# Where the masks and exponentials of an mLSTM head's decays are computed: in the core of the head before, or in the head's own key and value projection

## The chip, the cores and the metric

The kernel runs on one core of a Trainium2 chip. A core has five engines that run their own queues of instructions and wait for each other through semaphores: TensorE (PE, matrix products, with PEld for its weight loads), VectorE (DVE), ScalarE (ACT), GpSimd (POOL) and SyncE (SP), which here issues DMAs. ACT issues some DMAs too. The metric is the time of one execution on the device in microseconds (us). The profile is one execution, recorded instruction by instruction.

## The reference

One layer of a backbone over 1024 latent tokens with a prefix of 256 context tokens, width 1024. After a modulated norm, an input projection feeds two branches, a bidirectional mLSTM with 4 heads (keys and queries of 128, values of 256) and a windowed attention with 16 heads. Their outputs are projected, gated, merged and added to the input, and a convolutional feed-forward part follows. The change lies in the mLSTM. In each direction, with chunks of 128 tokens, a head computes

```
C_t = f_t C_{t-1} + i_t k_t v_t^T        n_t = f_t n_{t-1} + i_t k_t
h_t = C_t^T q_t / max(|n_t . q_t|, exp(-m_t))
```

In chunked form a chunk's output is the sum of two products. One is with the state C that the earlier chunks left. The other is inside the chunk: the scores S = k q^T, each multiplied by a decay exp(u_t + g_s), where u and g come from sums of the gates, and only for s up to t (from t on in the backward direction). The limit is a mask that adds a large negative number ahead of the exponential. Both directions are added, normed per head, and multiplied by a sigmoid gate.

## The kernel before

All matrix products are taken in three parts: each fp32 operand is split into a high half (copied by ACT, line 44) and a low half (the rest, by DVE, line 49), and `mm3` issues high x high, high x low and low x high (lines 91 to 93). Weights come in four loads of two row blocks each; a load goes to one of two raw buffers (`w1r`) and is split into `w1h` and `w1l`, of which there are five of each. SP issues the loads; a load waits until its raw buffer's former content has been split.

`stage_mlstm` works head by head. For head h:

- `proj_kv(h)` makes k and v for 10 chunks: two context chunks are loaded, eight latent ones are products with 8 row blocks (24 matmuls of 128x384 each), in one of two PSUM buffers. ACT evacuates k and the high half of v (`VH`), DVE the low half (`VL`).
- `trans_k` transposes k; `states` makes the first two state updates of each direction: `kwh` on POOL (line 941), `kwl` on DVE (942), the matmuls dC, the new state C on DVE (947, 949), and its halves `CH` (ACT) and `CL` (DVE).
- `turn(h-1)` transposes the former head's output (`mt`), scales it on ACT (`mo`, line 1042) and stores it; `proj_q` projects the queries (w_mlqo); `branch_sums` loads, adds and stores operands of later stages, with loads on ACT's queue and stores on SP's.
- `core(h)` makes S, multiplies it by the decays `ub` (DVE, line 977) and splits the result. Then, step by step, it updates the states and makes the outputs: the matmuls o (inside the chunk) and i (with the state), `nm` on ACT (992) and small operations on DVE (993 to 997), `hf` on POOL (999) the first time a chunk is reached and on DVE (1001) the second. Each of the states and outputs hangs on the one before through a chain over PE, DVE and ACT.
- `proj_o(h)` projects the output gate (the matmuls `mo` into the tiles `sg`). Its matmuls are placed among the core's, where PE would otherwise wait.
- `decays(h+1)` prepares the next head's four tiles `ub` of 128x512: a DMA of rows of u on SP's queue (917), the addition of the mask on POOL (922, one per tile) and four exponentials of 128x128 on ACT per tile (924).
- `readout(h)`: the sigmoid of `sg` on ACT (1023), squares of `hf` with their sums (1027, `rj`), two small POOL operations that end in a power (1028, 1029, `rr`), and hf * rr * sg on DVE (1032). This is done for two halves of the tokens.

Order on each engine: a scheduler lists all instructions ahead of time and picks, engine by engine, by the order in the program and by estimated times. `tc.issue_after(x)` pins what is written inside it behind the instruction x. In `decays` the additions of the masks are pinned behind `E.kw`, which is the last `kwh` of the core. The program's order around the change, at the end of `stage_mlstm`, is: core, proj_o, decays of the next head, readout, proj_kv of the next head.

Of the kernel before, what the change touches and what calls it, by code (L numbers as in the profile page):

```python
# [2 lines left out]

# [7 lines left out]
AF = mybir.ActivationFunctionType  # L11
ALU = mybir.AluOpType
# [11 lines left out]
NCB = NCTX // P  # L24
NBLK = NT // P
# [4 lines left out]
DQK = 128  # L30
# [12 lines left out]
def copy_act(nc, out, in_, scale=1.0):  # L43
    return nc.scalar.activation(out, in_, AF.Copy, scale=scale)  # L44
# [41 lines left out]
def mm3(nc, ps, lhs, rhs, ls, rs, start=True, stop=True):  # L86
    n = len(lhs)
    for i in range(n):
        lh, ll = lhs[i]
        rh, rl = rhs[i]  # L90
        nc.tensor.matmul(ps, lh[:, ls], rh[:, rs], start=start and i == 0, stop=False)  # L91
        nc.tensor.matmul(ps, lh[:, ls], rl[:, rs], start=False, stop=False)  # L92
        nc.tensor.matmul(ps, ll[:, ls], rh[:, rs], start=False, stop=stop and i == n - 1)  # L93


def sl(a, n):
    return slice(a, a + n)
# [3 lines left out]
def layer_kernel(ctx: ExitStack, tc: tile.TileContext, A: dict, out: bass.AP, dbg=None):  # L101
# [76 lines left out]
    with ExitStack() as st:  # L178
        stage_mlstm(E, st)
# [514 lines left out]
def stage_mlstm(E, st):  # L694
    nc, tc, A, ident, expo, hT, wts, dr = E.nc, E.tc, E.A, E.ident, E.expo, E.hT, E.wts, E.dr
# [26 lines left out]
    def orders(h):  # L722
        f = list(range(NBLK))
        bk = [1, 0] + list(range(NBLK - 1, NCB - 1, -1))
        return [(0, f), (1, bk)] if h % 2 == 0 else [(1, bk), (0, f)]

    def v_tiles(h, j, src):
        vh = vp.tile([P, DVA], F32R, tag="VH", name=f"VH{h}_{j}")
        vl = vp.tile([P, DVA], F32R, tag="VL", name=f"VL{h}_{j}")
        nc.gpsimd.tensor_copy(vh[:, DV:DVA], ones2[:, 0:2])  # L730
        nc.gpsimd.tensor_copy(vl[:, DV:DVA], ones2[:, 2:4])
        split_from(nc, vh[:, 0:DV], vl[:, 0:DV], src)
        return vh, vl

    def proj_kv(h):
        w = wts.load(A["w_ml"][h], 384)
        ks, vs = [None] * NBLK, [None] * NBLK
        for j in orders(h)[0][1]:
            k = kp.tile([P, DQK], F32, tag="k", name=f"k{h}_{j}")
            if j < NCB:  # L740
                nc.sync.dma_start(k, E.kx_d[j][:, h * DQK : (h + 1) * DQK])
                vr = kp.tile([P, DV], F32, tag="vr", name=f"vr{h}_{j}", bufs=2)
                nc.sync.dma_start(vr, E.vx_d[j][:, h * DV : (h + 1) * DV])
                vs[j] = v_tiles(h, j, vr)
            else:
                ps = mm_tile(f"kv{h}_{j}")
                mm3(nc, ps[:, :384], hT, w, sl((j - NCB) * P, P), sl(0, 384))
                copy_act(nc, k, ps[:, 0:DQK], scale=DQK ** -0.5)
                vs[j] = v_tiles(h, j, ps[:, 128:384])
            ks[j] = k  # L750
            if h == 0 and j - NCB in (0, 3):
                branch_sums()
        H.setdefault(h, {}).update(k=ks, V=vs)

    def proj_q(h):
        w = wts.load(A["w_mlqo"][h], 384)
        H.setdefault(h, {})["wqo"] = w
        qT = []
        for t in range(2):
            ps = mm_tile(f"q{h}_{t}")  # L760
            mm3(nc, ps, w, hT, sl(0, DQK), sl(t * 512, 512))
            qh, ql = b512(f"qh{h}_{t}"), b512(f"ql{h}_{t}")
            split_from(nc, qh, ql, ps)
            qT.append((qh, ql))
        H[h]["qT"] = qT

    def trans_k(h):
        kT = []
        for t in range(2):
            pt = tp_tile(f"kT{h}_{t}")  # L770
            for c in range(4):
                nc.tensor.transpose(pt[:, c * P : (c + 1) * P], H[h]["k"][NCB + 4 * t + c], ident)
            kh, kl = b512(f"kh{h}_{t}"), b512(f"kl{h}_{t}")
            split_from(nc, kh, kl, pt)
            kT.append((kh, kl))
        H[h]["kT"] = kT

    def proj_o(h):
        w = H[h]["wqo"]
        sgs = [rp.tile([P, 4, DV], F32, tag="sg", name=f"sg{h}_{t}", bufs=2) for t in range(2)]  # L780
        for cc in range(NB) if h % 2 else range(NB - 1, -1, -1):
            ps = mm_tile(f"mo{h}_{cc}")
            mm3(nc, ps[:, :DV], hT, w, sl(cc * P, P), sl(DQK, DV))

            fn = AF.Sigmoid if h == MLH - 1 else AF.Copy
            nc.scalar.activation(sgs[cc // 4][:, cc % 4], ps[:, :DV], fn)
        H[h]["sg"] = sgs

    GC = {}
# [117 lines left out]

    DM = {}

    def decays(h):  # L910

        for i in range(2):
            for d, _ in orders(h):
                t = i ^ d
                u = DM[h, t, d] = wp.tile([P, 4, P], F32, tag="ub", name=f"ub{h}_{t}_{d}", bufs=4)
                r0 = d * 64 + h * NBLK + NCB + 4 * (t if d == 0 else 1 - t)
                nc.sync.dma_start(
                    u.rearrange("p c t -> p (c t)"),
                    GC["u_d"][r0 : r0 + 4].rearrange("r t -> (r t)")[None, :].to_broadcast([P, 4 * P]),
                )  # L920
                with tc.issue_after(E.kw.ins):
                    nc.gpsimd.tensor_tensor(u, u, mlmask[:, d, None, :].to_broadcast([P, 4, P]), op=ALU.add)
                for c in range(4):
                    nc.scalar.activation(u[:, c], u[:, c], AF.Exp, bias=GC["col"]("g", r0 + c))

    EARLY = 2

# [88 lines left out]
    def halves(h):  # L1016
        return (1, 0) if h % 2 == 0 else (0, 1)

    def readout(h):
        hf, sgs = H[h]["hf"], H[h]["sg"]  # L1020
        for t in halves(h):
            if h < MLH - 1:
                nc.scalar.activation(sgs[t], sgs[t], AF.Sigmoid)
            rr = rp.tile([P, 8], F32, tag="rr", name=f"rr{h}_{t}", bufs=2)
            for c in range(4):
                junk = rp.tile([P, 512], F32, tag="mo", name=f"rj{h}_{t}_{c}", bufs=2)
                nc.scalar.activation(junk[:, :DV], hf[:, 4 * t + c], AF.Square, accum_out=rr[:, c : c + 1])
            nc.gpsimd.tensor_scalar(rr[:, 0:4], rr[:, 0:4], 1.0 / DV, EPS, op0=ALU.mult, op1=ALU.add)
            nc.gpsimd.tensor_tensor(rr[:, 4:8], rr[:, 0:4], expo[:, 0:4], op=ALU.pow)
            for c in range(4):  # L1030
                x = hf[:, 4 * t + c]
                E.turned = nc.vector.scalar_tensor_tensor(x, x, rr[:, 4 + c : 5 + c], sgs[t][:, c], op0=ALU.mult, op1=ALU.mult)
# [17 lines left out]
    def branch_sums():  # L1050
        n, i = SUMS.pop(0)
        two = [rp.tile([P, 4, DV], F32, tag="sg", name=f"{n}{i}_{j}", bufs=2) for j in range(2)]
        x, y, z, w = [t.rearrange("p c d -> p (c d)")[:, o : o + 512] for t in two for o in (0, 512)]
        tt = nc.vector.tensor_tensor
        if n[0] == "s":
            wb = A["w" + n[1:]]
            for o, src in ((x, wb[0, :, i]), (y, wb[1, :, i]), (z, wb[1, :, i + 4]), (w, wb[0, :, i + 4])):
                nc.scalar.dma_start(o, src)
            tt(z, y, z, op=ALU.add)
            tt(y, x, y, op=ALU.subtract)  # L1060
            tt(x, z, x, op=ALU.subtract)
            tt(w, w, x, op=ALU.subtract)
            res = z, x, y, w
        else:
            for o, r, t in ((x, i, 0), (y, i, 1), (w, i + 4, 0), (z, i + 4, 1)):
                nc.scalar.dma_start(o, E.attT_d[r * P : (r + 1) * P, t * 512 : (t + 1) * 512])
            tt(x, y, x, op=ALU.subtract)
            tt(y, z, y, op=ALU.subtract)
            tt(z, z, x, op=ALU.subtract)
            tt(w, w, z, op=ALU.subtract)  # L1070
            res = x, z, y, w
        for j, o in enumerate(res):
            nc.sync.dma_start(E.sums_d[n][:, j, i], o)
# [3 lines left out]
    wp = st.enter_context(tc.tile_pool(name="mlw", bufs=2, reuse_waits="tile"))  # L1077
    rp = st.enter_context(tc.tile_pool(name="mlr", bufs=2, reuse_waits="tile"))
    proj_kv(0)
    trans_k(0)  # L1080
    states(0)
    proj_q(0)
    decays(0)
    for h in range(MLH):
        core(h)
        proj_o(h)
        if h + 1 < MLH:
            decays(h + 1)
        readout(h)
        if h + 1 < MLH:  # L1090
            proj_kv(h + 1)
            trans_k(h + 1)
            states(h + 1)
        turn(h)
        if h + 1 < MLH:
            proj_q(h + 1)
            for _ in range((3, 4, 3)[h]):
                branch_sums()
# [844 lines left out]
```

## Time and profile before

| | us |
|---|---|
| median of three runs | 1932.23 |
| lowest, highest | 1932.02, 1933.36 |
| profiled execution | 1930.5 |
| its span | 1928.7 |
| PE busy in the span | 1889.6 |
| core of head 0, 1, 2, 3 (first S matmul to last mo matmul) | 47.2, 47.7, 46.8, 44.9 |

The mean clock that PE was granted was 0.998 of the full one. A row of the profile is one of two kinds. In a row of the timeline stand the start in us from the start of the span, the duration, the engine, the line, the operation, the output tile and its inputs, their shapes, and how many such instructions were merged; brackets show how long the engine was idle just before and what ended that. In a row of stretches stand its start and end, its length, the busy time of PE, PEld, DVE, ACT and POOL with counts of instructions, the granted clock, the share of DMA and GB/s.

### The profile page before, as it was taken

Reading aid. Unit: us, or ns where it says so; the run is one execution under the profiler, and the core shown is the slowest. Engines: PE = TensorE matmul, PEld = TensorE weight load, DVE = VectorE, ACT = ScalarE, POOL = GpSimd, SP = SyncE. Lnnn points to the kernel's source line nnn. Section 1 sums busy time; section 2 is a strip of 40 time slices with the busy share of each in tenths; the row PEclk is TensorE's granted clock in tenths of the full one; section 3 lists DMA queues with packets and bytes.
Section 4 is the critical chain, followed back from the end, with each engine's and each line's share of the span. In section 5 each row is a group of like instructions: output and inputs, shape, how many; then the busy total and the mean of one; then the engine's idle time right before and its main releaser. Section 6 shows DMA issues by size and latency. Waiting matters only on the chain.

```text
span 1928.7 us, 28748 instructions
## 1 busy us (share of the span) xinstructions
PE 1889.6 (98%) x10012; PEld 1628.6 (84%) x10012; DVE 1441.0 (75%) x2886; ACT 994.9 (52%) x1979; POOL 328.0 (17%) x534
## 2 busy tenths in 40 slices
PE   7999999999999999999999999999999999999999
PEld 3988888888888889999999888888888888888887
DVE  3767768777678666666667878679988888897564
ACT  4835656555546445353537556256544445455441
POOL 1223333433333233131211012010000000000000
PEclk9999999999999999999999999999999999999999
DMA  9632222313222323435326982722354544499851
GB/s 352 202 121 65 67 72 61 96 58 97 58 64 82 124 87 112 137 105 183 97 99 227 379 298 86 281 83 88 131 207 175 196 163 176 160 325 347 300 166 66
DMA packets 139378, 298.54 MB, mean 155 GB/s; under 512 B 15440, under 2 KB 39648, under 8 KB 136416
## 3 DMA queue, kind: packets, MB, share of 16 engines
q1 hardware_dynamic: 124832, 270.48, 40.6%
q10 hardware_dynamic: 14400, 26.22, 4.1%
q8 instruction: 79, 1.29, 0.3%
q14 instruction: 67, 0.55, 0.1%
HBM read 220.55 MB, written 76.10 MB: 154 GB/s over the span
## 4 chain that ended last, share of the span: by engine, by line
PE 82%; DVE 6%; DMA 4%; ACT 4%; POOL 2%; issue 2%; SPq 0%; POOLq 0%; ACTq 0%; DVEq 0%
PE pa L1525 4%; PE pa L1526 4%; PE pa L1527 4%; PE pt L632 3%; PE g L93 3%; PE g L92 3%; PE g L91 3%; PE yb L1525 2%; PE yb L1526 2%; PE yb L1527 2%; PE dx L1527 2%; PE dx L1525 2%; PE dx L1526 2%; PE pb L1526 2%; PE pb L1527 2%; PE pb L1525 2%
## 5 line engine op out<-in xcount | busy, mean ns | idle before, releaser
L613 POOL TENSOR_SCALAR P<-P,st 128x640 f32<-128x640 f32 (+1 forms) x128 | 111.6, 891 | 236.0 <-DVE st L611 113.6
L44 ACT ACTIVATE ph<-pt 128x512 fp32r<-128x512 f32 x152 | 88.1, 598 | 75.3 <-PE pt L632 72.7
L600 DVE CUSTOM_DVE_ANT_0 P<-s,maskA,nsink 128x640 f32<-128x640 f32 (+1 forms) x112 | 103.2, 921 | 18.3 <-PE s L597 16.5
L604 ACT ACTIVATE P<-P,st 128x640 f32<-128x640 f32 (+1 forms) x128 | 102.4, 800 | 8.8 <-DVE st L600 8.4
L49 DVE TENSOR_TENSOR pl<-pt,ph 128x512 fp32r<-128x512 f32 x152 | 100.0, 685 | 6.6 <-ACT ph L44 6.6
L91 PE MATMUL g<-hH,fh 128*128 128x512 f32 x256 | 103.2, 403 | 0.0
L92 PE MATMUL g<-hL,fh 128*128 128x512 f32 x256 | 102.5, 400 | 0.0
L93 PE MATMUL g<-hH,fl 128*128 128x512 f32 x256 | 100.7, 393 | 0.6 <-DVE fl L49 0.6
L632 PE MATMUL pt<-ident,P 128*128 128x128 f32 x608 | 93.2, 274 | 3.9 <-POOL P L613 3.2
L632 PEld LDWEIGHTS pt<-ident,P 128*128 128x128 f32 x608 | 72.8, 140 | 18.7 <-POOL P L613 7.0
L91 PE MATMUL kv<-w1h,hH 128*128 128x384 f32 x256 | 86.3, 338 | 1.3 <-ACT w1h L44 1.3
L91 PE MATMUL pq<-w1h,hH 128*128 128x384 f32 (+1 forms) x256 | 87.0, 340 | 0.0
L92 PE MATMUL pq<-w1l,hH 128*128 128x384 f32 (+1 forms) x256 | 86.7, 339 | 0.3 <-DVE w1l L49 0.3
L93 PE MATMUL pq<-w1h,hL 128*128 128x384 f32 (+1 forms) x256 | 86.9, 339 | 0.0
L92 PE MATMUL kv<-w1l,hH 128*128 128x384 f32 x256 | 86.5, 338 | 0.0
L93 PE MATMUL kv<-w1h,hL 128*128 128x384 f32 x256 | 86.3, 337 | 0.0
L91 PE MATMUL mo<-w1h,hH 128*128 128x256 f32 x256 | 72.0, 281 | 0.0
L941 POOL TENSOR_SCALAR kwh<-k,gcall 128x128 fp32r<-128x128 f32 x72 | 31.7, 445 | 236.7 <-PE dC L92 185.1
L93 PE MATMUL mo<-w1h,hL 128*128 128x256 f32 x256 | 71.8, 281 | 0.0
L92 PE MATMUL mo<-w1l,hH 128*128 128x256 f32 x256 | 71.7, 280 | 0.0
L1663 ACT ACTIVATE cv<-ua,vecT 128x1024 f32<-128x1024 f32 x22 | 27.4, 1245 | 82.2 <-DVE ua L1636 82.2
L1525 PE MATMUL dx<-dwh,dfh 128*128 128x512 f32 x176 | 68.7, 390 | 0.0
(587 smaller groups left out, 6373.0 us busy)
## 6 DMA issues: line engine op xcount, KB each, us to landing
ur<-in_w_up SPq DMA_DIRECT2D x22, 1024.0 KB, 4.9
wmb<-in_w_modB SPq DMA_DIRECT2D x48, 256.0 KB, 2.9
f_d<-cv SPq DMA_DIRECT2D x22, 512.0 KB, 2.7
wm<-in_w_modA SPq DMA_DIRECT2D x16, 512.0 KB, 10.2
fr<-in_w_g SPq DMA_DIRECT2D x32, 256.0 KB, 3.3
drf<-fs_d SPq DMA_DIRECT2D x15, 512.0 KB, 7.0
drw<-wt_d SPq DMA_DIRECT2D x14, 512.0 KB, 6.0
w1b<-in_w_cx SPq DMA_DIRECT2D x16, 388.0 KB, 5.0
```

The costliest lines, as they stand in the source:

```text
L44: return nc.scalar.activation(out, in_, AF.Copy, scale=scale)
L49: (nc.vector if eng == "v" else nc.gpsimd).tensor_tensor(lo, src, hi.bitcast(F32), op=ALU.subtract)
L91: nc.tensor.matmul(ps, lh[:, ls], rh[:, rs], start=start and i == 0, stop=False)
L92: nc.tensor.matmul(ps, lh[:, ls], rl[:, rs], start=False, stop=False)
L93: nc.tensor.matmul(ps, ll[:, ls], rh[:, rs], start=False, stop=stop and i == n - 1)
L600: nc.vector.tensor_tensor_reduce(pm[:, :W], ps[:, off : off + W], mask[:, :W], scale=ss[:, h : h + 1], scalar=nsink[:, hh : hh + 1], op0=A ...
L604: nc.scalar.activation(pm[:, :W], pm[:, :W], AF.Exp, bias=st4[:, h : h + 1], scale=-1.0, accum_out=st4[:, 4 + h : 5 + h])
L613: nc.gpsimd.tensor_scalar(Ps[h][:, :W], Ps[h][:, :W], st4[:, 12 + h : 13 + h], 1.0, op0=ALU.mult, op1=ALU.mult)
L632: nc.tensor.transpose(pt[:, h * P : (h + 1) * P], Ps[h][:, kb * P : (kb + 1) * P], ident)
L1525: nc.tensor.matmul(ps, lh, rh, start=start and i == 0, stop=False, skip_group_check=True)
L1526: nc.tensor.matmul(ps, lh, rl, start=False, stop=False, skip_group_check=True)
L1527: nc.tensor.matmul(ps, ll, rh, start=False, stop=stop and i == n - 1, skip_group_check=True)
```

## The change

The function `decays(h)` is split. `masked(h)` keeps the DMAs and the mask additions; the new `decays(h, pin)` holds the exponentials alone, inside a pin that the caller gives. For head 0, both are called one after the other where `decays(0)` was, with no pin on the exponentials. For the other heads, `masked(h+1)` is written behind `readout(h)`, and `E.kw` is set by the readout's power, so that the additions are pinned behind the last power instead of the last `kwh`. The exponentials are written inside `proj_kv(h+1)`, at the sixth chunk in its order (two context chunks, then the fourth latent one), and are pinned behind the evacuation of that chunk's k. Lines of the changed kernel have other numbers: the masks 922 become 924, the exponentials 924 become 934, and lines behind them go up by 10.

```diff
-                copy_act(nc, k, ps[:, 0:DQK], scale=DQK ** -0.5)
+                kc = copy_act(nc, k, ps[:, 0:DQK], scale=DQK ** -0.5)
                 vs[j] = v_tiles(h, j, ps[:, 128:384])
             ks[j] = k
+            if h and j == orders(h)[0][1][5]:
+                decays(h, tc.issue_after(kc.ins))
...
-    def decays(h):
+    def masked(h):
 
         for i in range(2):
             for d, _ in orders(h):
...
                 with tc.issue_after(E.kw.ins):
                     nc.gpsimd.tensor_tensor(u, u, mlmask[:, d, None, :].to_broadcast([P, 4, P]), op=ALU.add)
-                for c in range(4):
-                    nc.scalar.activation(u[:, c], u[:, c], AF.Exp, bias=GC["col"]("g", r0 + c))
+
+    def decays(h, pin):
+        with pin:
+            for i in range(2):
+                for d, _ in orders(h):
+                    t = i ^ d
+                    r0 = d * 64 + h * NBLK + NCB + 4 * (t if d == 0 else 1 - t)
+                    u = DM[h, t, d]
+                    for c in range(4):
+                        nc.scalar.activation(u[:, c], u[:, c], AF.Exp, bias=GC["col"]("g", r0 + c))
...
-            nc.gpsimd.tensor_tensor(rr[:, 4:8], rr[:, 0:4], expo[:, 0:4], op=ALU.pow)
+            E.kw = nc.gpsimd.tensor_tensor(rr[:, 4:8], rr[:, 0:4], expo[:, 0:4], op=ALU.pow)
...
-    decays(0)
+    masked(0)
+    decays(0, nullcontext())
     for h in range(MLH):
         core(h)
         proj_o(h)
+        readout(h)
         if h + 1 < MLH:
-            decays(h + 1)
-        readout(h)
+            masked(h + 1)
         if h + 1 < MLH:
             proj_kv(h + 1)
             trans_k(h + 1)
```

The order on POOL at the end of head 0's core, before. The names are tile names: `kwh0_1_8` is head 0, direction 1, step 8, and `ub1_1_1` is a tile of head 1's decays; the last number is the buffer's.

```order
L941 TENSOR_SCALAR kwh0_1_8_8458<-k0_3_7643,gcall_7540 128x128
L922 TENSOR_TENSOR ub1_1_1_8741<-ub1_1_1_8741,mlmask_7417 128x512
L922 TENSOR_TENSOR ub1_0_0_8748<-ub1_0_0_8748,mlmask_7417 128x512
L922 TENSOR_TENSOR ub1_0_1_8755<-ub1_0_1_8755,mlmask_7417 128x512
L922 TENSOR_TENSOR ub1_1_0_8762<-ub1_1_0_8762,mlmask_7417 128x512
L730 COPY VH1_4_9037<-ones2_7419 128x2
```

And on POOL at the end of head 0's readout, now.

```order
L1038 TENSOR_SCALAR rr0_0_8758<-rr0_0_8758 128x4
L1039 TENSOR_TENSOR rr0_0_8758<-rr0_0_8758,expo_62 128x4
L924 TENSOR_TENSOR ub1_1_1_8773<-ub1_1_1_8773,mlmask_7417 128x512
L924 TENSOR_TENSOR ub1_0_0_8776<-ub1_0_0_8776,mlmask_7417 128x512
L924 TENSOR_TENSOR ub1_0_1_8779<-ub1_0_1_8779,mlmask_7417 128x512
L924 TENSOR_TENSOR ub1_1_0_8782<-ub1_1_0_8782,mlmask_7417 128x512
L951 TENSOR_SCALAR kwh1_0_1_9160<-k1_1_8809,gcall_7540 128x128
```

The four additions moved from behind the core's last `kwh` to behind the readout's last power. Ahead of them now also stand some copies of ones into `VH` and `VL` and three of the next head's `kwh`, which stood behind them before.

On ACT, near step 8 of head 0's core, before:

```order
L924 ACTIVATE ub1_1_1_8741<-ub1_1_1_8741,gcall_7540 128x128
L44 ACTIVATE CH0_0_7_8398<-C0_0_0_7914 128x258
L924 ACTIVATE ub1_1_1_8741<-ub1_1_1_8741,gcall_7540 128x128 x3
L924 ACTIVATE ub1_0_0_8748<-ub1_0_0_8748,gcall_7540 128x128
L44 ACTIVATE CH0_1_7_8411<-C0_1_0_7924 128x258
L924 ACTIVATE ub1_0_0_8748<-ub1_0_0_8748,gcall_7540 128x128 x2
L992 ACTIVATE nm0_0_8_8479<-i0_0_8_8475,gcall_7540 128x257
```

And on ACT in head 1's key and value projection, now:

```order
L44 ACTIVATE k1_6_8928<-kv1_6_8929 128x128
L44 ACTIVATE VH1_6_8955<-kv1_6_8929 128x256
L934 ACT_TABLE_LOAD
L934 ACTIVATE ub1_1_1_8773<-ub1_1_1_8773,gcall_7540 128x128 x4
L934 ACTIVATE ub1_0_0_8776<-ub1_0_0_8776,gcall_7540 128x128 x4
L934 ACTIVATE ub1_0_1_8779<-ub1_0_1_8779,gcall_7540 128x128 x4
L934 ACTIVATE ub1_1_0_8782<-ub1_1_0_8782,gcall_7540 128x128 x4
L44 ACTIVATE k1_5_8977<-kv1_5_8978 128x128
L44 ACTIVATE VH1_5_9004<-kv1_5_8978 128x256
L1076 DMA t_at0_0_9315<-attT_d_64 128x512 x2
```

The exponentials were scattered among the core's own work and are now one block between the evacuations of two chunks, with a load of ACT's function table ahead of it, and the loads of a branch sum behind it. Loads of the table: two stood ahead of exponentials in the cores of heads 1 and 2; now one stands ahead of the exponentials in each of the three projections, and a new one stands in head 3's core ahead of the first sigmoid of its gate (line 788). The orders of DVE and of SP's loads of weights and of u rows are the same around these places.

More of the change, by code (lines that the diff above doesn't have):

```diff
@@ L1 @@
 import math
-from contextlib import ExitStack
+from contextlib import ExitStack, nullcontext
 import concourse.bass as bass
```

## The prediction

> **What bounds the kernel now.** I read the totals first, then the stretches of the four heads, then the waits inside them.
>
> ```profile
> PE 1889.6 (98%) x10012; PEld 1628.6 (84%) x10012; DVE 1441.0 (75%) x2886; ACT 994.9 (52%) x1979; POOL 328.0 (17%) x534
> ```
>
> TensorE (PE) is busy 98% of the span of 1928.7 us, and the change neither adds nor removes a matmul. So it can only move the 39 us in which PE is idle, and each of its steps counts by what it does to an idle gap of PE. The next view gives, per head, the stretch from the first S matmul to the last mo matmul: stretch, length, then busy time of PE, PEld, DVE, ACT, POOL.
>
> ```profile
> 704.40:751.60 47.20, 44.18 (x356) 42.75 (x355) 39.22 (x131) 29.91 (x80) 21.80 (x46) 1.00 0.13 40
> 801.40:849.10 47.70, 45.16 (x356) 43.13 (x355) 38.61 (x129) 29.93 (x80) 20.91 (x46) 1.00 0.11 32
> 899.50:946.30 46.80, 44.31 (x356) 42.83 (x355) 38.63 (x129) 30.38 (x79) 20.06 (x40) 1.00 0.12 35
> 996.20:1041.10 44.90, 44.29 (x357) 43.00 (x356) 36.09 (x129) 22.33 (x61) 11.33 (x23) 1.00 0.28 98
> ...
> 728.00:734.00 6.00, 3.67 (x28) 3.28 (x27) 5.93 (x13) 3.37 (x11) 6.00 (x7) 1.00 0.01 3
> 826.00:833.00 7.00, 5.07 (x37) 4.32 (x36) 7.00 (x15) 4.32 (x10) 7.00 (x10) 1.00 0.01 4
> 923.00:930.00 7.00, 5.11 (x38) 4.41 (x36) 6.94 (x17) 4.31 (x10) 7.00 (x11) 1.00 0.01 4
> 1018.00:1025.00 7.00, 7.00 (x58) 6.67 (x57) 6.73 (x30) 3.44 (x9) 1.65 (x4) 1.00 0.01 2
> ```
>
> Heads 0 to 2 leave PE idle for 3.02, 2.54 and 2.49 us, head 3 for 0.61. Most lies in one place, near step 8: 2.33, 1.93 and 1.89 us, where POOL is busy without a gap; in head 3, which has no next head and so no masks, the same place has none. POOL's rows there, then DVE's in head 0, then two of PE's waits:
>
> ```profile
> 728.19 5.40 POOL L922 TENSOR_TENSOR ub<-ub,mlmask 128x512 f32<-128x512 f32 x4
> 826.62 5.44 POOL L922 TENSOR_TENSOR ub<-ub,mlmask 128x512 f32<-128x512 f32 x4
> 923.14 5.23 POOL L922 TENSOR_TENSOR ub<-ub,mlmask 128x512 f32<-128x512 f32 x4
> ...
> 727.23 0.34 DVE L942 SCALAR_TENSOR_TENSOR kwl<-k,gcall,kwh 128x128 fp32r<-128x128 f32 x1
> 727.49 0.47 DVE L1001 SCALAR_TENSOR_TENSOR hf<-nm,hf 128x256 f32<-128x256 f32 x1
> 728.58 1.03 DVE L942 SCALAR_TENSOR_TENSOR kwl<-k,gcall,kwh 128x128 fp32r<-128x128 f32 x1
> 729.54 1.51 DVE L1001 SCALAR_TENSOR_TENSOR hf<-nm,hf 128x256 f32<-128x256 f32 x1
> 730.97 1.48 DVE L49 TENSOR_TENSOR CL<-C,CH 128x258 fp32r<-128x258 f32 x1
> 732.38 0.47 DVE L949 SCALAR_TENSOR_TENSOR C<-C,dec,dC 128x258 f32<-128x258 f32 x1
> ...
> 733.00 0.36 PE L91 MATMUL dC<-VH,kwh 128*128 128x258 f32 x1 [1.88 <-DVE C L949]
> 832.89 0.36 PE L91 MATMUL i<-CH,qh 128*128 128x258 f32 x1 [1.18 <-DVE nm L996]
> ```
>
> While the masks run, a DVE instruction with two inputs in SBUF lasts until the running mask has ended: kwl 1.03 for 0.34, hf 1.51 for 0.47. One that reads PSUM keeps its time (C, 0.47). The chain of small operations on DVE then runs late, and PE waits for dC and i.
>
> **The change part by part.** *The masks leave the core.* POOL's order has them behind the last pow of the readout instead of behind the last kwh. The three gaps, 2.33 + 1.93 + 1.89 = 6.2 us, lose their cause. Head 3's place shows the end of a core without them at zero idle; I leave 0.3 us as not recovered, since head 3 has other work (other transfers and no next weights) around it. Bounds: a gain of 4.3 (if each place keeps the 0.61 that head 3's whole stretch has) to 6.2.
>
> *The masks arrive at the start of the next key and value projection.* They are the same four instructions of some 1.35 us, 5.4 in a row, and hold DVE in the same way. What stands there (pow of the readout, then DVE, ACT, PE):
>
> ```profile
> 746.25 1.12 POOL L1029 TENSOR_TENSOR rr<-rr,expo 128x4 f32<-128x4 f32 x1
> 846.09 1.12 POOL L1029 TENSOR_TENSOR rr<-rr,expo 128x4 f32<-128x4 f32 x1
> 942.35 1.13 POOL L1029 TENSOR_TENSOR rr<-rr,expo 128x4 f32<-128x4 f32 x1
> ...
> 750.41 1.83 DVE L49 TENSOR_TENSOR w1l<-w1r,w1h 128x768 fp32r<-128x768 f32 x2 [2.77 <-ACT w1h L44]
> 848.51 1.83 DVE L49 TENSOR_TENSOR w1l<-w1r,w1h 128x768 fp32r<-128x768 f32 x2 [1.44 <-ACT w1h L44]
> 851.20 1.67 DVE L1032 SCALAR_TENSOR_TENSOR hf<-hf,rr,sg 128x256 f32<-128x256 f32 x4
> 853.79 1.96 DVE L49 TENSOR_TENSOR w1l<-w1r,w1h 128x768 fp32r<-128x768 f32 x2 [0.92 <-ACT w1h L44]
> 945.12 1.83 DVE L49 TENSOR_TENSOR w1l<-w1r,w1h 128x768 fp32r<-128x768 f32 x2 [2.12 <-ACT w1h L44]
> ...
> 754.68 0.84 ACT L44 ACTIVATE w1h<-w1r 128x768 fp32r<-128x768 f32 x1 [1.55 <-DMA w1r<-in_w_ml]
> ...
> 755.58 0.61 PE L91 MATMUL kv<-w1h,hH 128*128 128x384 f32 x2 [0.31 <-ACT w1h L44]
> 853.81 0.44 PE L91 MATMUL kv<-w1h,hH 128*128 128x384 f32 x1 [0.66 <-ACT w1h L44]
> ```
>
> The masks would run from 747.4, 847.2 and 943.5 to about 752.8, 852.6 and 948.8, over the two w1l of each head. The first w1l frees one of two raw buffers; only then does SP issue the third load of w_ml, whose landing starts w1h (754.68), for which PE already waits 0.31 to 0.66 us. So a delay of the first w1l goes to PE whole. A held instruction waits 0 to 1.3 us, by where in a mask it falls; the middle is 0.65. I take 0.65 for heads 0 and 2. Between heads 1 and 2, DVE has the second w1l, a sum, a VL and four hf queued ahead of the third w1l, which had 0.92 us to spare; two or three of these would be held by a mask, so I take 1.3. Together +2.6, with bounds of 0 (each first w1l between two masks) and 8 (two masks ahead of it in each head, 2.6 x 3).
>
> *The sixteen exponentials move into the projection.* They were spread over ACT's work at the end of a core, and now run as a block behind the fourth latent chunk's evacuation, with a table load ahead of them.
>
> ```profile
> L924 ACT ACTIVATE ub<-ub,gcall x64: 385/388/407, 693.1 to 935.3; 128x128 f32<-128x128 f32 x64
> ...
> 734.37 1.27 ACT L924 ACTIVATE ub<-ub,gcall 128x128 f32<-128x128 f32 x4
> ...
> 741.18 1.28 ACT L1023 ACT_TABLE_LOAD   x1
> 742.48 1.06 ACT L1023 ACTIVATE sg<-sg 128x1024 f32<-128x1024 f32 x1
> ...
> 769.12 0.28 ACT L44 ACTIVATE k<-kv 128x128 f32<-128x128 f32 x1 [3.64 <-PE kv L93]
> 769.29 0.38 ACT L44 ACTIVATE VH<-kv 128x256 fp32r<-128x256 f32 x1
> 781.70 0.28 ACT L44 ACTIVATE k<-kv 128x128 f32<-128x128 f32 x1 [3.64 <-PE kv L93]
> ```
>
> One exponential takes 0.388 us, four overlapped 1.27, so sixteen some 4.9, and with the load 6.1. From 769.7 they end at 775.8. The evacuations at 769.12 and 781.70 are three chunks apart, so PE takes 4.2 us a chunk; the next chunk, done at 773.3, is evacuated 2.5 us late, its VH by 776.5 and its VL on DVE by 777.0. Its PSUM bank, one of two, is wanted again at 777.5, when the chunk between is done: 0.5 us is left. Cost 0, with PE's work on that chunk as the cover. The masks' results are wanted here, 16 us after the last mask, so this wait stays free too; on POOL itself the next head's last early kwh is queued behind the masks, and PE reads it only after the projection. If the exponentials don't overlap (0.388 x 16 = 6.2 for 4.9), the block ends 1.3 later and PE waits 0.8 per head, 2.4 in all. In the order, the two loads ahead of exponentials in the cores of heads 1 and 2 become three in the projections; PE waited for neither, so no gain in the cores.
>
> [...] The row shows the load, 1.28, and the sigmoid 0.02 behind it; no drain stands in these rows. [...]
>
> *What is queued behind the block on ACT* are the loads of the branch sums (t_at, s_bm). Their sums on DVE, and the stores on SP, come up to 2.5 us later, and SP's loads of w_mlqo stand behind such stores. Those feed w1h on ACT, ahead of the evacuation of the transposed output:
>
> ```profile
> 787.97 0.84 ACT L44 ACTIVATE w1h<-w1r 128x768 fp32r<-128x768 f32 x1
> 788.72 1.25 ACT L1042 ACTIVATE mo<-mt,mlw 128x512 f32<-128x512 f32 x2
> ```
>
> That w1h has no idle ahead of it, so some of the delay is free. I take +0.5 in all three heads together, between 0 and 2.5 (the delay once in full).
>
> *A new table load in head 3's core*, ahead of its first sigmoid gate: ACT is 22.33 busy of 44.90 there. I take +0.3, between 0 and the 1.28 of its row. SP's four loads of u rows keep their place in its order, among the first of a core, 40 us ahead of the masks; cost 0.
>
> **The sum.** -6.2 + 0.3 + 2.6 + 0 + 0.5 + 0.3 = -2.5 us. Against the profiled execution's 1930.5 us (span 1928.7) that is 1928.0. The median of the runs is 1.7 above the profiled one, so the median comes to 1932.2 - 2.5 = 1929.7. A measurement of this kernel can tell about 0.2%, 3.9 us, from no change: the forecast lies within it, on the faster side.
>
> **Rivals.** *The start of the projection absorbs the masks.* Each w1l falls between two masks, or the readout comes so early (ACT has 4.9 us less to do ahead of its squares) that most masks are over before the first w1l. For it speaks that DVE was idle 2.77, 1.44 and 2.12 ahead of these w1l; against it that they start only 3.0, 1.3 and 1.6 us after the pow's end, less than 5.4, and that the squares wait for the core's last hf, which comes from PE. Then -6.2 + 0.3 and at most 0.5: -5.6, or 1926.6.
>
> *DVE is late by more than a mask.* The masks leave DVE one turn each: a VL, the last hf of the first half and a sum stand ahead of or between the w1l, and each takes a turn, so that the load of the third weights slips by two or three masks in each head. With the other 0.8 us it cancels the gain at 1.7 us per head (5.1 / 3) and decides for slower, by the bound above, at 3.0 (9.0 / 3). At 3.3 it gives +4.8, or 1937. Against it: rows of the core show three DVE turns in 5.4 us, and at the new place only VL is ready ahead of the first w1l.
>
> *The block on ACT stalls the projection.* If ACT stands still behind the load for as long as the load itself, 1.28, the block ends 1.3 later and PE waits 0.8 in each head, as with exponentials that don't overlap: 2.4 more, net -0.1, or 1932.1. Against it stand 1.27 for four, and the 0.02 behind the load at 741.18. [...]
>
> **How the numbers follow.** Forecast 0.37; absorbed masks 0.36; stalled block 0.09; DVE late 0.18. Faster is the second, 0.36; within the bound are the first and third, 0.46; slower is the last, 0.18. The range leaves out the best of the second (below -6.2: 1926.0) and the upper half of the last: 1926.0 to 1935.5. Taken alone, the forecast reaches from 1928.4 to 1932.
>
> **What would show it.** Right: near step 8 of heads 0 to 2, kwl at 0.34 and hf at 0.47, and PE's 6.2 us of waits gone; four masks behind the pow, a w1l of 1.2 to 2 us for 0.92, and PE's wait for w1h grown from 0.3 to 0.7 to about 1 to 2. In the projections a block of 6.1 us on ACT, with no PE wait behind it. Wrong: a PE wait for ACT's k or VH in the chunks after the block; a wait at another place of the core of the same size as the one removed; or w1l at its 0.92 with no mask over it.

## The result and the profile after

| | kernel before | changed kernel |
|---|---|---|
| median, first comparison | 1932.63 us | 1925.89 us (6 runs, 1923.57 to 1926.89) |
| ratio, with its 95% interval | 1 | 0.9965 [0.9955, 0.9976] |
| ratio of a second comparison (below) | 1 | 0.9961 [0.9948, 0.9973] |
| profiled execution, its span | 1930.5, 1928.7 | 1926.05, 1924.3 |

The changed kernel is faster by 6.7 us in the first comparison. The forecast was 2.5, and the time lies 0.1 us below the predicted range. The two profiled executions differ by 4.4 us only; the experiments show why the medians differ by more.

The totals of the page, after:

```profile
PE 1887.4 (98%) x10012; PEld 1626.8 (85%) x10012; DVE 1438.2 (75%) x2886; ACT 998.4 (52%) x1981; POOL 328.5 (17%) x534
```

The stretches of the four heads' cores, and then the places near step 8 of heads 0 to 2. The columns are those of the stretches before: start and end, length, busy time of PE, PEld, DVE, ACT, POOL, granted clock, DMA.

```profile
705.20:749.60 44.40, 43.71 (x356) 42.61 (x355) 36.40 (x130) 25.33 (x64) 20.20 (x46) 1.00 0.15 43
800.00:844.90 44.90, 44.30 (x356) 42.91 (x355) 36.37 (x130) 24.73 (x64) 19.21 (x45) 1.00 0.13 36
896.90:940.90 44.00, 43.39 (x356) 42.48 (x355) 35.73 (x128) 24.73 (x62) 19.12 (x40) 1.00 0.13 37
991.10:1036.60 45.50, 44.65 (x357) 42.99 (x356) 36.98 (x129) 23.34 (x62) 11.64 (x23) 1.00 0.29 101
...
728.00:732.30 4.30, 4.30 (x36) 4.16 (x35) 4.13 (x17) 2.37 (x8) 1.34 (x5) 1.00 0.01 4
824.00:829.00 5.00, 5.00 (x44) 5.00 (x44) 4.72 (x22) 2.27 (x5) 2.80 (x9) 1.00 0.02 5
919.00:924.00 5.00, 5.00 (x42) 4.86 (x42) 4.84 (x22) 2.66 (x8) 1.51 (x6) 1.00 0.01 3
```

PE no longer stops near step 8. The stretches are 2.8 us shorter in each of heads 0 to 2 (47.20, 47.70 and 46.80 before), and 0.6 longer in head 3 (44.90 before). DVE's operations there run at their own length (kwl 0.33, hf 0.48):

```profile
729.31 0.33 DVE L952 SCALAR_TENSOR_TENSOR kwl<-k,gcall,kwh 128x128 fp32r<-128x128 f32 x1
729.56 0.48 DVE L1011 SCALAR_TENSOR_TENSOR hf<-nm,hf 128x256 f32<-128x256 f32 x1
```

At the start of the next projection the masks (POOL) stand over the two w1l (DVE) of each head, as forecast, and PE waits behind them:

```profile
745.08 5.77 POOL L924 TENSOR_TENSOR ub<-ub,mlmask 128x512 f32<-128x512 f32 x4
...
748.40 3.27 DVE L49 TENSOR_TENSOR w1l<-w1r,w1h 128x768 fp32r<-128x768 f32 x2 [3.36 <-ACT w1h L44]
843.75 3.74 DVE L49 TENSOR_TENSOR w1l<-w1r,w1h 128x768 fp32r<-128x768 f32 x2 [2.04 <-ACT w1h L44]
939.71 3.27 DVE L49 TENSOR_TENSOR w1l<-w1r,w1h 128x768 fp32r<-128x768 f32 x2 [3.36 <-ACT w1h L44]
...
753.97 0.61 PE L91 MATMUL kv<-w1h,hH 128*128 128x384 f32 x2 [0.57 <-ACT w1h L44]
847.54 0.44 PE L92 MATMUL kv<-w1l,hH 128*128 128x384 f32 x1 [0.37 <-DVE w1l L49]
849.75 0.61 PE L91 MATMUL kv<-w1h,hH 128*128 128x384 f32 x2 [0.55 <-ACT w1h L44]
851.69 0.44 PE L92 MATMUL kv<-w1l,hH 128*128 128x384 f32 x1 [0.80 <-DVE w1l L49]
945.20 0.62 PE L91 MATMUL kv<-w1h,hH 128*128 128x384 f32 x2 [0.50 <-ACT w1h L44]
```

Two w1l take 3.27 to 3.74 us instead of 1.83. PE's waits there sum to 0.57, 1.72 and 0.50 us. The block of exponentials in head 1's projection:

```profile
768.07 1.28 ACT L934 ACT_TABLE_LOAD   x1
769.37 4.21 ACT L934 ACTIVATE ub<-ub,gcall 128x128 f32<-128x128 f32 x14
...
773.78 0.39 ACT L934 ACTIVATE ub<-ub,gcall 128x128 f32<-128x128 f32 x1
774.07 0.26 ACT L44 ACTIVATE k<-kv 128x128 f32<-128x128 f32 x1
775.89 0.28 ACT L44 ACTIVATE k<-kv 128x128 f32<-128x128 f32 x1 [1.29 <-PE kv L93]
```

It lasts 6.1 us, and the second evacuation behind it is waiting for PE again, so PE waited for neither.

For the experiments I read each trace by stages: from the start of a head's first S matmul to the start of the next projection's first matmul (core), from there to the next first S (projection), for head 3 up to the first transposing matmul of its output, and from there to the end (rest). What lies ahead of head 0's core is left out; it varies between 703.6 and 706.8 us. All in us:

| trace | cores 0, 1, 2 | core 3 | projections 1, 2, 3 | rest |
|---|---|---|---|---|
| before, as profiled | 47.04, 47.54, 46.68 | 44.75 | 49.96, 50.51, 50.04 | 887.8 |
| changed | 44.27, 44.78, 43.88 | 45.33 | 50.51, 52.13, 50.34 | 887.9 |
| changed, again | 44.32, 44.79, 43.94 | 45.42 | 50.39, 51.39, 50.91 | 887.8 |
| exponentials only | 47.13, 47.26, 46.88 | 45.41 | 50.04, 49.59, 50.22 | 887.9 |
| masks in quarters | 46.37, 46.87, 46.09 | 44.73 | 50.23, 51.12, 50.23 | 887.8 |
| masks twice | 47.13, 47.31, 48.31 | 45.31 | 50.69, 51.37, 50.34 | 887.8 |
| sigmoid early | 44.28, 44.75, 44.01 | 44.80 | 50.26, 51.23, 50.44 | 893.2 |
| masks later | 44.27, 44.76, 44.00 | 45.35 | 50.05, 50.32, 50.07 | 893.4 |
| masks later, same layout | 44.26, 44.78, 43.88 | 44.97 | 50.18, 52.97, 50.22 | 888.3 |
| later masks and sigmoid | 44.26, 44.78, 43.93 | 44.76 | 50.19, 49.80, 50.69 | 887.8 |
| before, with a spare tile | 48.15, 49.01, 46.70 | 44.79 | 50.05, 51.28, 50.13 | 895.1 |
| before, trace 2 | 48.14, 49.02, 46.70 | 44.76 | 50.04, 52.06, 50.61 | 887.8 |
| before, trace 3 | 48.14, 47.55, 46.69 | 44.71 | 50.17, 50.68, 50.03 | 887.8 |
| before, trace 4 | 48.04, 49.00, 46.67 | 44.74 | 50.10, 51.09, 50.17 | 887.9 |

### The profile page after: what moved, and what is told of

Read it like the earlier page. It is cut to its first block, busy times and chain, and to the rows that moved or that the text cites. A ratio compares the mean times of both kernels' runs of the same rounds, so it can differ in the third digit from the quotient of the medians.

```text
span 1924.3 us, 28724 instructions
## 1 busy us (share of the span) xinstructions
PE 1887.4 (98%) x10012; PEld 1626.8 (85%) x10012; DVE 1438.2 (75%) x2886; ACT 998.4 (52%) x1981; POOL 328.5 (17%) x534
## 4 chain that ended last, share of the span: by engine, by line
PE 84%; DVE 5%; DMA 3%; ACT 3%; POOL 2%; issue 2%; POOLq 0%; SPq 0%; ACTq 0%; DVEq 0%
PE pa L1536 4%; PE pa L1537 4%; PE pa L1538 4%; PE pt L632 3%; PE g L93 3%; PE g L92 3%; PE g L91 3%; PE yb L1536 2%; PE yb L1538 2%; PE yb L1537 2%; PE dx L1538 2%; PE dx L1536 2%; PE dx L1537 2%; PE pb L1537 2%; PE pb L1536 2%; PE pb L1538 2%
## 5 line engine op out<-in xcount | busy, mean ns | idle before, releaser
L604 ACT ACTIVATE P<-P,st 128x640 f32<-128x640 f32 (+1 forms) x128 | 102.4, 800 | 8.9 <-DVE st L600 8.5
```

What stands on the lines that cost most here:

```text
L604: nc.scalar.activation(pm[:, :W], pm[:, :W], AF.Exp, bias=st4[:, h : h + 1], scale=-1.0, accum_out=st4[:, 4 + h : 5 + h])
```

## The experiments

### Which part brings the gain

The exponentials alone in the projection, with the masks left in the core (edit against the changed kernel):

```diff
-            E.kw = nc.gpsimd.tensor_tensor(rr[:, 4:8], ...
+            nc.gpsimd.tensor_tensor(rr[:, 4:8], ...
...
         proj_o(h)
-        readout(h)
         if h + 1 < MLH:
             masked(h + 1)
+        readout(h)
```

> Only the exponentials move into the projection; the mask additions stay in the core, behind its last kwh. Theory 1 (while a mask runs on POOL, DVE's instructions with two inputs in SBUF stand still, and that alone stretches the core): the stretches from the first S matmul to the next projection's first matmul stay at 47.0, 47.6 and 46.7 us, the waits near step 8 stay, the waits for w1h at the projection's start go back to 0.3, 0.7 and 0.3, and the time is 1932 to 1934. Theory 2 (the exponentials and their table loads on ACT delay nm, CH and the readout at the core's end): the stretches fall to 44.3 to 44.9 as in the changed kernel, and the time is 1924 to 1925. In between, each has its share.

Measured: 1932.24 us, ratio 0.9999 [0.9991, 1.0008]. The cores of heads 0 to 2 keep their length. Moving the exponentials gains nothing there, as theory 1 says. PE's waits for w1h at the three starts are 0.44, 0.44 and 0.50 us, not the 0.3, 0.7 and 0.3 that I expected.

Then the other way round, the changed kernel with the masks added a second time, in the core (`add_masks` issues the four additions alone):

```diff
         proj_o(h)
+        if h + 1 < MLH:
+            masked(h + 1)
         readout(h)
         if h + 1 < MLH:
-            masked(h + 1)
+            add_masks(h + 1)
```

> The changed kernel with the mask additions done twice, once in the core as before and once behind the readout as now (a second addition of 0 or -1e30 leaves the result). Theory: the POOL instructions in the core alone cause the stop near step 8 and what follows it; then the three stretches go back to 47.0 to 48.1, 47.5 to 49.0 and 46.7 us, and the time to the changed kernel's plus 8.3 to 11: 1933.5 to 1936. The lower ends are without, the higher with a drop of PE's granted clock behind the stop, which two of the three traces of the kernel before show in head 0. Rival: the stop needs the exponentials on ACT as well; then the stretches stay under 46 and the time at 1926 to 1929.

Measured: 1934.38 us, ratio 1.0006 [0.9997, 1.0015]. The whole gain is gone, with the exponentials still in the projection. So four POOL instructions in each of three cores cost them what the change gains there: 142.75 us for the three, against 132.93. The sizes are as expected in heads 0 and 1; in head 2 the stretch is 1.6 longer than expected, with PE's granted clock at 0.50 for 3.4 us in it (on that, below).

### How POOL holds DVE

The kernel before, each mask cut into four:

```diff
-                    nc.gpsimd.tensor_tensor(u, u, mlmask[:, d, None, :].to_broadcast([P, 4, P]), op=ALU.add)
+                    for c in range(4):
+                        nc.gpsimd.tensor_tensor(u[:, c], u[:, c], mlmask[:, d], op=ALU.add)
```

> The kernel before, with each mask addition of 128x512 on POOL cut into four of 128x128, at the same place. Theory 1 (DVE is held to the end of the one running POOL instruction): the longest hold falls from 1.3 to about 0.4 us, kwl and hf take 0.4 to 0.9 instead of 1.0 to 1.5, the three core stretches fall by 1.5 to 2.5 us each, and the time is 1925 to 1928. [...]

Measured: 1929.35 us, ratio 0.998 [0.9971, 0.999]. The timeline of POOL and DVE near step 8 of head 0:

```profile
728.81 7.81 POOL L923 TENSOR_TENSOR ub<-ub,mlmask 128x128 f32<-128x128 f32 x16
...
729.21 0.63 DVE L943 SCALAR_TENSOR_TENSOR kwl<-k,gcall,kwh 128x128 fp32r<-128x128 f32 x1
729.76 0.67 DVE L1002 SCALAR_TENSOR_TENSOR hf<-nm,hf 128x256 f32<-128x256 f32 x1
730.41 0.63 DVE L49 TENSOR_TENSOR CL<-C,CH 128x258 fp32r<-128x258 f32 x1
...
733.84 0.39 PE L93 MATMUL dC<-VH,kwl 128*128 128x258 f32 x1 [0.25 <-DVE kwl L943]
```

The three held operations take 0.63, 0.67 and 0.63 us (1.03, 1.51 and 1.48 before) beside POOL instructions of 0.47 to 0.66 us; in the kernel before each of the three ended 0.14 to 0.28 us behind the end of a mask of 1.28 to 1.45. The hold goes by the length of one POOL instruction. But the stretches fall by 0.6 to 0.7 us each, not 1.5 to 2.5, and the time is between the 1925 to 1928 of the theory and the 1932.65 of the kernel before beside it. Sixteen additions take 7.81 us instead of 5.40, and more of DVE's operations fall under them. One quarter takes 0.47 us (median of 64), more than a quarter of a whole mask's 1.30 (median in the changed kernel), and 0.64 to 0.66 where it stands beside a held hf or CL: the hold goes both ways. In the projection of the changed kernel too, a mask beside a w1l takes up to 2.02 us. The mechanism was right and my size was off: a shorter hold is paid more often. Against the mean of four traces of the kernel before (142.8 us, below) the three cores gain 3.5 us, near the 3.3 between the medians.

### What the masks cost at their new place, and the table load in head 3

The masks of the changed kernel held until the second latent chunk's k is there:

```diff
+    late = mp.tile([P, 1], F32, name="late")
...
+            if h and j == orders(h)[0][1][3]:
+                E.kw = nc.gpsimd.tensor_copy(late, k[:, 0:1])
+                add_masks(h)
             if h and j == orders(h)[0][1][5]:
                 decays(h, tc.issue_after(kc.ins))
...
```

> The changed kernel, with the mask additions of heads 1 to 3 held on POOL until the second latent chunk's k has been evacuated (a POOL copy of one column of that k stands ahead of them), so that the splits of the projection's weights have passed. If the masks over the w1l cost what the trace of the changed kernel shows (waits at the projection's start of 0.6, 1.7 and 0.5 instead of 0.3, 0.7 and 0.3), the time falls by 1.5, to about 1924.4, w1l takes 0.92, and no wait of PE arises at the new place, since only VL is split there on DVE and it reads PSUM. Rival: the waits for w1h stay, because the weights' loads and not DVE set them, and the time stays at 1925.9.

And one small sigmoid behind head 3's exponentials:

```diff
+    sink = mp.tile([P, 1], F32, name="sink")
...
+            if h == MLH - 1:
+                nc.scalar.activation(sink, ones[:, 0:1], AF.Sigmoid)
```

> The changed kernel, with one sigmoid of 128x1 behind head 3's exponentials, so that the table load for the sigmoid gates of head 3 is done in its projection and not in its core. If that load is what made head 3's core 0.6 us longer (45.5 for 44.9), the core goes back to 44.9 and the time falls by 0.6, to about 1925.3, provided that the longer block on ACT (1.3 more) costs the projection nothing; by the slack worked out before, it would cost up to 0.8 there. Rival: the 0.6 is something else, and the core stays at 45.5.

Measured: masks later 1929.84 us, 0.9988 [0.9979, 0.9997]; sigmoid early 1931.58 us, 0.9996 [0.9988, 1.0005]. Both are far slower than expected, while the stages that they aim at do what was expected: the projections of the first are at 50.05, 50.32 and 50.07, and head 3's core in the second is at 44.80 for 45.33. The loss is in the rest, 893.4 and 893.2 us for 887.9. Each adds a tile of 4 bytes per partition to a pool that opens ahead of others. So the later masks were tried again, and then both edits together, with columns of a tile that is no longer read, and that one suspected cause by itself:

```diff
-                E.kw = nc.gpsimd.tensor_copy(late, k[:, 0:1])
+                E.kw = nc.gpsimd.tensor_copy(zz[:, 0:1], k[:, 0:1])
...
-                nc.scalar.activation(sink, ones[:, 0:1], AF.Sigmoid)
+                nc.scalar.activation(zz[:, 1:2], ones[:, 0:1], AF.Sigmoid)
```

```diff
     ones = mp.tile([P, P], F32, name="onesm")
+    spare = mp.tile([P, 1], F32, name="spare")
+    nc.gpsimd.memset(spare, 0.0)
```

> The changed kernel itself, word for word, beside the next three on one chip. If its gain is a property of the program, 1925 to 1927, 0.996 to 0.997 of the kernel before; if it was the luck of its six runs, up to 1932, as the two variants with one small tile more had.

> The run with the later masks again, but the POOL copy writes into a column of a tile that is no longer read, so that no tile of 4 bytes is added to the pool of the mLSTM stage. Theory: that tile moved the buffers of the next stage and made its start wait 4 to 5 us (0.96 and 3.11 for bawh and baah); without it the stretch after the last transpose takes 887.9 as in the changed kernel, and the time is 1924 to 1924.5, the changed kernel's less 1.5 to 2.5 for the projections. Rival: the later masks themselves delay the next stage; then it stays at 893 and the time at 1929.8.

> The later masks and the early sigmoid together, both without a new tile. If both savings are on the path and independent: 1.5 to 2.5 in the projections and 0.5 in head 3's core below the changed kernel, 1923 to 1924. Rival: the sum is given back at the start of the next stage, whose transfers then come later against PE; 1925 to 1926.

> The kernel before with one tile of 4 bytes per partition added to the pool of the mLSTM stage and cleared once, nothing else. If the layout alone delays the next stage's first loads, the stretch after the last transpose grows from 887.8 to about 893 and the time to 1937. Rival: the delay in the two variants came from their other edits, and the time stays at 1932.6.

| | us | ratio to before |
|---|---|---|
| changed, again | 1925.05 | 0.9961 [0.9948, 0.9973] |
| masks later, same layout | 1922.57 | 0.9947 [0.9934, 0.9961] |
| later masks and sigmoid | 1923.29 | 0.9952 [0.994, 0.9965] |
| before, with a spare tile | 1940.28 | 1.0042 [1.0029, 1.0054] |

The spare tile alone costs 7 us. The trace shows where: the first rows are SP's loads for the next stage in the kernel before, the second in the one with the tile, and then PE's waits in it.

```profile
1024.74 4.78 SPq L1227 DMA_DIRECT2D bawr<-in_w_ba  x2
```

```profile
1051.89 1.70 SPq L1229 DMA_DIRECT2D bawr<-in_w_ba  x2
...
1049.21 0.50 PE L1527 MATMUL yb<-baah,bawh 128*128 128x512 f32 x1 [0.96 <-ACT bawh L44]
1061.66 2.07 PE L1527 MATMUL yb<-baah,bawh 128*128 128x512 f32 x4 [3.65 <-ACT baah L44]
```

Two loads of the next stage come 27 us later (22 us, counted from the end of head 3's core), and its first matmuls wait. That their buffers now lie on memory which the mLSTM stage still uses is my estimate from these rows; no run shows the addresses. I had expected 893 us for the rest and 1937 in all, but the rest takes 895.1: behind the wait of 3.65 us PE's granted clock is at 0.50 for 3.4 us, and the four matmuls of the last row take 2.07 us, where the same four in the run with the early sigmoid took 1.21.

Without the tile, the later masks leave the w1l alone. In the run with both edits, the two w1l are back at 1.83 us, the masks run behind them, and PE's waits at the three starts are 0.38, 0.44 and 0.48 for 0.57, 1.72 and 0.50, so the saving lies mostly in the middle one. The first start:

```profile
758.72 5.03 POOL L934 TENSOR_TENSOR ub<-ub,mlmask 128x512 f32<-128x512 f32 x4
...
747.85 1.83 DVE L49 TENSOR_TENSOR w1l<-w1r,w1h 128x768 fp32r<-128x768 f32 x2 [3.35 <-ACT w1h L44]
...
753.09 0.62 PE L91 MATMUL kv<-w1h,hH 128*128 128x384 f32 x2 [0.38 <-ACT w1h L44]
```

But the masks can hold other work at their later place. In the trace of the later masks alone they stand over sums of the branches (`t_at`) in the second projection, a VL is queued behind those, and PE waits for it (such a sum takes 0.69 us without a mask beside it):

```profile
855.19 5.94 POOL L934 TENSOR_TENSOR ub<-ub,mlmask 128x512 f32<-128x512 f32 x4
...
855.22 1.81 DVE L1089 TENSOR_TENSOR t_at<-t_at,t_at 128x512 f32<-128x512 f32 x1
857.07 1.67 DVE L1090 TENSOR_TENSOR t_at<-t_at 128x512 f32<-128x512 f32 x1
858.66 0.41 DVE L49 TENSOR_TENSOR VL<-kv,VH 128x256 fp32r<-128x256 f32 x1
...
859.12 0.45 PE L91 MATMUL kv<-w1h,hH 128*128 128x384 f32 x1 [0.78 <-DVE VL L49]
864.68 0.46 PE L91 MATMUL kv<-w1h,hH 128*128 128x384 f32 x1 [1.11 <-DVE VL L49]
```

That projection takes 52.97 us, the longest of all, and this was the slowest of its five runs (1927.13). So "no wait of PE arises at the new place" was wrong for this run; the other two traces with later masks have no wait for a VL. The second wait follows an evacuation that came late on ACT, behind three issues of DMAs; what held those is open.

Head 3's core is at 44.76 in the run with both edits, so the table load was its 0.6 us. (With the later masks alone, and the load in place, it shows 44.97, and the rest is 0.5 longer.) The medians of both versions lie about 2 us below the changed kernel's beside them, near the two terms (some 2 for the masks, below, and 0.6), but the intervals overlap: that they beat it is likely and not shown. The sigmoid added nothing that the medians show.

### Why the medians differ by more than the first two traces

The kernel before once more, for its trace alone, three times in all:

> The kernel before, word for word, for a second trace of it: the two traces at hand differ by 4.4 us in the span while the medians differ by 6.7 and 8.2. If the first trace was a lucky one of its kernel, this one has a span of 1929.5 to 1932, and the stage in which it is longer is one in which DMAs vary; the waits in the cores are the same to 0.1 us, with stretches of 47.0, 47.5 and 46.7. If the 4.4 is the whole change, the span is 1928 to 1929.

> The same once more, a third trace of the kernel before: a span between 1928 and 1932, core stretches of 47.0, 47.5 and 46.7 to 0.2 us if nothing on a core's path depends on DMAs.

> A fourth trace of the kernel before, for the granted clock of PE behind the stop near step 8. If the drop of the clock to about 0.5 for 3 us belongs to that stop, it shows in head 0 or 1 in at least every second trace of kernels with the masks in the core, and in none without them; the stretch is then 48.1 instead of 47.0 in head 0, 49.0 instead of 47.5 in head 1.

Measured: spans of 1934.3, 1930.2 and 1933.7 us. The first trace was the shortest of four. I expected the longer ones to be longer where DMAs vary, and the cores to stay. But half or more of the difference is in the cores: 2.6 of 5.6, 1.1 of 1.5 and 2.4 of 5.0 us. Three us behind the stop near step 8 of head 0 (733.5 to 736.5), in the first trace, in traces 2, 3 and 4:

```profile
733.50:736.50 3.00, 3.00 (x26) 2.93 (x25) 2.74 (x14) 2.86 (x9) 3.00 (x12) 1.00 0.00 0
```

```profile
733.50:736.50 3.00, 2.72 (x13) 2.75 (x14) 2.10 (x12) 2.06 (x7) 2.50 (x7) 0.50 0.00 0
...
835.50:838.50 3.00, 3.00 (x18) 3.00 (x17) 3.00 (x12) 2.99 (x10) 1.09 (x5) 0.55 0.00 0
```

```profile
733.50:736.50 3.00, 3.00 (x17) 3.00 (x16) 2.03 (x11) 2.22 (x8) 2.50 (x10) 0.53 0.00 0
```

```profile
733.50:736.50 3.00, 2.01 (x9) 2.04 (x10) 2.81 (x13) 1.34 (x4) 2.83 (x6) 0.59 0.00 0
```

The granted clock, third number from the end, is 1.00 in the first trace and 0.50 to 0.59 in the others. Head 0's core starts at the same time in the first trace and in trace 3, but 0.8 and 1.6 us later in traces 2 and 4, so only trace 3 shows the same work: PE is busy as in the first, but does 17 matmuls for 26. Head 0's core then takes 48.1 us instead of 47.0, and head 1's, where it happens too (0.55 behind its stop in trace 2), 49.0 instead of 47.5. Over the traces of kernels with whole masks in the core (four of before, the spare tile, the exponentials only, the masks twice), the drop is in head 0's core in four of seven, in head 1's in three, in head 2's in one. In the six traces of kernels without masks in these cores there is none, and in the one with quartered masks none either.

Why one trace has the drop and the next has not is not shown; I have an estimate, worked out from the drops themselves. Each of these eight is at 0.50 and lasts 3.41 us, and in traces 2 and 4 the second begins 102.4 us behind the first, thirty such lengths. So I cut the time into lengths of 3.41 us counted from a drop; in the first trace, which has none in the cores, from its two drops in the first 50 us (at 32.06 and 49.13, five such lengths apart). The same stop of 1.88 us (731.1 to 733.0), in the first trace and then in trace 3:

```profile
728.38:731.80 3.42, 2.29 (x17) 1.86 (x15) 3.42 (x5) 2.03 (x7) 3.42 (x3) 1.00 0.02 5
731.80:735.21 3.41, 2.21 (x17) 2.19 (x18) 3.15 (x14) 2.22 (x7) 3.41 (x8) 1.00 0.00 0
735.21:738.62 3.41, 3.41 (x29) 3.21 (x28) 3.41 (x11) 3.32 (x11) 1.92 (x8) 1.00 0.01 2
```

```profile
730.29:733.70 3.41, 1.53 (x13) 1.36 (x13) 3.41 (x6) 1.85 (x7) 3.41 (x4) 1.00 0.00 0
733.70:737.11 3.41, 3.41 (x18) 3.41 (x18) 2.44 (x13) 2.63 (x8) 2.91 (x11) 0.50 0.00 0
```

In the first trace an edge falls into the stop, and PE is busy for 2.2 to 2.3 us of each of the two lengths. In trace 3 the stop lies inside one, 1.53 us are left, and the next length is at 0.50. Ahead of seven of the eight drops PE was busy for 1.46 to 1.71 us of a length, ahead of the eighth for 2.08; the emptiest length in these cores without a drop behind it has 2.04. So my estimate is that for the same stop the place of the edges decides whether it costs a drop. Busy time alone does not separate the two: in the next stage of the run with the masks later, a length with 1.49 us has no drop behind it, and the first of the early drops in the first trace follows one with 2.20. The longest single stop ahead of a drop in the cores is 1.88 us, and in the run with the masks twice it is 0.82.

## Why the prediction was wrong

The direction was right, and so was the mechanism on both sides: masks that hold DVE in the core, and the same masks over the w1l in the projection. The case that came is near the rival of absorbed masks in time (1926.6), but not for its reason, since the masks were not absorbed: they hit every first pair of w1l. The step that failed is the first term of the sum, "the three gaps, 2.33 + 1.93 + 1.89 = 6.2 us, lose their cause", and with it the bound "to 6.2" that closed the range below: the masks cost the three cores 8.3 us in the trace at hand, and 9.8 on the mean of four.

- *The gain in the cores.* Forecast 5.9 us, with at most 6.2. The first two traces show 8.3 (47.04 + 47.54 + 46.68 less 44.27 + 44.78 + 43.88). The gaps went to zero as said, which is 6.15 of it; PE's busy time in these stretches fell too, by 0.47, 0.86 and 0.92 us, which I had taken as fixed. A matmul of 128x256 is recorded with 0.28 us and followed by the next after 0.12, so a stop hides up to 0.16 us of itself behind the last matmul's record, and a shorter one shows no gap. The starts bear this out: the time between PE's starts beyond the usual distance (0.12 us for 256 columns, 0.11 for 128) sums to 15.8 us over the three cores before and 7.5 after, so it falls by 8.3 where the gaps fall by 6.15. Against the mean of four traces of the kernel before (142.8 for three cores) the gain is 9.8, the rest being the drops of the clock, which one trace could not show. The 1.7 us by which the median lay above the profiled execution hinted at them; the prediction carried it through as a constant.
- *The masks at the new place.* Forecast +2.6. PE's waits at the three starts grew by 0.26, 1.06 and 0.19, together 1.5 (0.57 + 1.72 + 0.50 less 0.31 + 0.66 + 0.31). Heads 0 and 2 were sized at 0.65 each; the first w1l came late enough in a mask that it waited little. The 1.3 between heads 1 and 2 was near. By length the masks cost more than these waits. The second projection also holds waits of PE at the transposes of the former head's output, for `kl` on DVE or `mo` on ACT, which vary from run to run: 0.45, 2.03, 0.63 and 1.26 us in the four traces of the kernel before, 0.71 and none in the changed one. Without them the three projections take 151.9 to 152.7 us in the four traces with the masks over the w1l (changed twice, early sigmoid, masks twice), and 149.7 to 150.7 in nine without, the two traces of later masks without a wait for VL among them. That is 2.1 on the means, of which the idle column shows 1.5: the forecast was nearer than the waits say.
- *The exponentials, 0.* Right, as the block of 6.1 us without a wait of PE and the run with them alone show. The first exponential starts 0.02 us behind the load of 1.28 us, so the standstill that the rival of a stalled block supposed does not show.
- *What is queued behind the block, +0.5.* No cost shows. In head 1 the w1h ahead of the evacuation of mo now waits 0.49 us for its load where it had no wait. But PE's waits at the transposes, just there, did not grow (0.71 us and none, for 0.45 to 2.03 before), and the run with the exponentials alone, with the same block and the same loads behind it, has none; its projections take 149.9 us in all.
- *The table load in head 3, +0.3.* It cost 0.6: 45.33 and 45.42 with it, 44.76 and 44.80 with the load moved ahead.

By stages, the mean of two traces of the changed kernel differs from the mean of four before by -9.8 in the cores of heads 0 to 2, +1.5 in the projections (+2.1 by the masks, and less waiting at the transposes), +0.6 in head 3's core and -0.3 ahead of head 0's core, where nothing was changed: -8.0 in all. The first two traces alone give -8.3 + 2.5 + 0.6 + 0.8 = -4.4. The two comparisons of medians give -6.7 and -8.2. So the gain does not rest on one pair of traces; that the first comparison came out just 0.1 us below the range is chance.

## What to carry to other kernels

Price a stop of a pipelined engine by the distance between the starts of its instructions, or by the length of the stage beside one without the stop, not by the idle column alone (here the gaps of 6.15 us stood for 8.3). Where PE stops for a microsecond or two in an otherwise full stretch, look at the granted clock behind the stop in more than one trace before taking one trace's span as the kernel's (here it fell to 0.50 for 3.41 us behind eight stops in the cores, in five of seven traces, and behind none in the first). When a variant is slower in a stage that its edit doesn't touch, look at that stage's first loads, and try the edit again without the tile it added (here one tile cost 7 us).

## What the runs showed that I had not expected

- PE's granted clock fell to 0.50 for 3.41 us behind a stop of 0.8 to 1.9 us, in some runs of a kernel and not in others, and cost 1.0 to 1.6 us each time. That the edges of lengths of 3.41 us beside the stop make the difference is my estimate.
- One more tile of 4 bytes per partition in a pool that opens early cost 7 us (1.0042 [1.0029, 1.0054]), by loads of a later stage that were issued 27 us later.
- Four times as many POOL additions on a quarter of the data each took 7.81 us instead of 5.40 while DVE worked beside them.
- At a later place the masks held sums on DVE instead of the w1l, and in one trace PE waited 0.78 us for a VL behind them.
